# The LRU's gates from high and low halves in fp32r, three tiles of mLSTM's convolution and the chain of softplus placed among them, and the row of x's factors one step later

## The chip, the cores and the metric

One NeuronCore of a Trainium2 chip runs the whole program. The metric is the device time of one execution in microseconds, as the median over the runs. TensorE (PE) multiplies matrices; VectorE (DVE), ScalarE (ACT) and GpSimd (POOL) work element by element; SyncE (SP) issues nearly all DMA transfers.

## The reference

One layer of a decoder trunk with 256 tokens of width 2048. `h = RMSNorm(x)`, then one projection `h @ w_in`, whose columns feed three groups of heads:

```
xc = causal_conv4(xb)                          # A: RG-LRU, 512 channels in 4 blocks of 128
r  = sigmoid(block_diag(xc, wa) + ba)          # recurrence gate
i  = sigmoid(block_diag(xc, wx) + bx)          # input gate
log_a = -8 * r * softplus(-lam)
a, u = exp(log_a), sqrt(-expm1(2 * log_a)) * (i * xc)
h_t = a_t * h_(t-1) + u_t;   y_lru = h * silu(zb)

uc = silu(causal_conv4(u))                     # B: mLSTM, 768 channels, 4 heads
q, k = block_diag(uc, wq), block_diag(uc, wk);  v = block_diag(u, wv)
...                                            # gates, stabilised matrix memory, norm
...                                            # C: MoBA attention, 768 channels, 6 heads
```

The three outputs are joined, projected by `w_out` and added to `x`; then cross-attention into 256 memory tokens, and a final RMSNorm. All tensors are float32.

## The kernel before, in words

**Weights.** The weight columns are cut into groups (`GROUPS`), and each group into chunks along the 2048 inputs (`CHUNKS`, numbered on through the program): lx is chunks 0 to 7, u0 8 to 11, u2 12 to 15, u4 16 to 19, lz0 20 to 23, o0 24 to 31, o1 32 to 39, lz2 40 to 43, then q, k and the rest. `load` (L162) issues a chunk's DMA on SP's queue into one of four `raw` buffers. `split` (L179) makes two fp32r halves of it: ACT copies the high half `wh` (L204), DVE subtracts it from `raw` for the low half `wl` (recorded at L150, in the helper `tt`). Six buffers hold each half. `mm` (L252) multiplies the chunk: for the groups of channels (lx, u, lz, q, k) a matmul of `wh` with x's high and low halves side by side, 512 columns (L272), and one of `wl` with x's high half, 256 columns (L276); for o, z and v three matmuls with the weights as the moving operand (L292 to L294).

**Order.** The main loop (L1193) goes chunk by chunk: it first records the splits of chunks up to four ahead, with the loads that follow, then `mm(i)`, then what hangs on a finished group (`done`, L1128), then one `step` of a queue of generators. Each generator is a piece of the work beside the projections; it runs up to its next `yield` in one step, so a `yield` decides behind which chunk's matmuls the next piece stands. `done` puts evacuations in front of the queue and other work behind it. Each engine executes its own instructions in the recorded order, and waits on the others by semaphores.

**The work that the change touches.** After lx the queue holds two empty steps, `stats("x")` (L432), `lru_scale`, `u_scale`, `softplus_lam` and `lru_core`. `stats` makes the factors `1/rms` of the tokens, as two diagonal matrices `d_x` (DVE, L450), two steps later multiplies them with ones on PE (L455) so that a row of factors stands in every partition (`rrow`), and `lru_scale` (L501) and `u_scale` (L576) multiply the LRU's input and u0 by it on POOL. `softplus_lam` (L392) is a small Exp on ACT and a chain of some 18 short dependent operations on DVE (`log1p`, L376). `lru_core` (L508) convolves four tiles of 128 channels, one per step: an Identity on ACT with the first tap and the bias (L512), three multiply-adds on DVE (recorded at L153, helper `stt`). Then it makes the gates: per tile two f32 matmuls on PE, with `lw`, whose DMA is issued at chunk 6 (L519, L520), and two Sigmoids, two tiles per step; then Exp and Tanh, the products, a Sqrt and the scans. `ml_conv` (L580) is the same convolution for mLSTM, six tiles in six steps, queued when u4 is done; then three Silu, two empty steps, and `ml_qkv`.

Of the kernel before, what the change touches and what calls it, by code (L numbers as in the profile page):

```python
# [9 lines left out]
F32 = mybir.dt.float32  # L10
# [96 lines left out]
def kernel(ctx: ExitStack, tc: tile.TileContext, xT, memT, x, mem, ws, vec_d, lw_d, fg_d, out):  # L107
# [234 lines left out]
    def expand(name, blk):  # L342
        t = bdp.tile([128, 6, 128], F32, name=f"bd_{name}", tag="bd")
        bd[name] = t
        for c in range(6):
            G.tensor_tensor(t[:, c, :].rearrange("p (b o) -> p b o", o=4), dmask,
                            blk(c)[:, None, :].to_broadcast([128, 32, 4]), OP.mult)

    def late_consts():
        G.memset(dmask, 1.0)  # L350
# [40 lines left out]

    def softplus_lam():  # L392
        lam = vc("lam", 0, 4)
        e, m = small("sp_e", 4), small("sp_m", 4)
        stt(e, lam, -1.0, lam, OP.mult, OP.max)
        S.activation(e, e, AF.Exp, scale=-1.0)
        log1p(sp8, e, "sp")
        V.tensor_scalar(m, lam, -1.0, 0.0, op0=OP.mult, op1=OP.max)
        tt(sp8, sp8, m, OP.add)
        V.tensor_scalar(sp8, sp8, 8.0, None, op0=OP.mult)  # L400
        V.tensor_scalar(nsp8, sp8, -1.0, None, op0=OP.mult)
# [30 lines left out]
    def stats(which):  # L432
# [18 lines left out]
        yield  # L451
        yield
        p = ps()
        for i in range(2):
# [46 lines left out]
    def lru_scale():  # L501
        xp = L["xp"]
        for b in range(2):
            v = xp[:, 2 * b:2 * b + 2, 3:259]
            G.tensor_tensor(v, v, rb("x"), OP.mult)
        yield

    def lru_core():  # L508
        xp = L["xp"]
        xc = big(2, 4, 256)  # L510
        for c in range(4):
            S.activation(xc[:, c, :], xp[:, c, 0:256], AF.Identity, scale=vc("cw", 4 * c), bias=vc("cb", c))  # L512
            for j in range(1, 4):
                stt(xc[:, c, :], xp[:, c, j:j + 256], vc("cw", 4 * c + j), xc[:, c, :], OP.mult, OP.add)
            yield
        r, ig = big(3, 4, 256), big(4, 4, 256)
        for c in range(4):
            p = ps()
            P.matmul(p[:, :256], lw[:, c, :], xc[:, c, :], start=True, stop=True)  # L519
            P.matmul(p[:, 256:], lw[:, 4 + c, :], xc[:, c, :], start=True, stop=True)  # L520
            S.activation(r[:, c, :], p[:, :256], AF.Sigmoid, bias=vc("ba", c))
            S.activation(ig[:, c, :], p[:, 256:], AF.Sigmoid, bias=vc("bx", c))
            if c % 2:
                yield
        aa, th = big(5, 4, 256), big(6, 4, 256)
        for c in range(4):
            S.activation(aa[:, c, :], r[:, c, :], AF.Exp, scale=nsp8[:, c:c + 1])
            S.activation(th[:, c, :], r[:, c, :], AF.Tanh, scale=sp8[:, c:c + 1])
            if c % 2:
                yield  # L530
        tt(r, aa, aa, OP.mult)
# [554 lines left out]
    def bg(*gens):  # L1086
        queue.extend(gens)
# [105 lines left out]
    for i in range(NS):  # L1193
# [94 lines left out]
```

## Time and profile before

| what | value |
|---|---|
| median of 3 runs | 517.29 us (517.17 to 517.47) |
| the profiled execution's own time | 518.01 us |
| its span, first to last instruction | 516.3 us |
| PE busy | 505.4 us, 98% of the span, 2682 matmul passes |
| DVE busy | 345.5 us, 67% |
| ACT busy | 301.0 us, 58% |
| POOL busy | 62.7 us, 12% |
| mean granted TensorE clock | 0.997 |
| read from HBM | 96.15 MB, 190 GB/s over the span |

Times in the profile count from the first instruction. The profiled execution is one execution; its own time is 0.72 us over the median of the runs. A share of busy time is a mean over stages: where PE is busy without a break, the other engines' idle time costs nothing; what counts for them is whether a result is there when PE's next matmul wants it.

### The profile page before, as it was taken

The numbers are of one execution on the slowest core, as the hardware profiler recorded it, in microseconds if no ns is written. First come the engines' busy times: TensorE is split into PE (matmuls) and PEld (weight loads), VectorE is DVE, ScalarE is ACT, GpSimd is POOL, SyncE is SP. The second block draws the span as 40 slices with busy tenths as digits, with TensorE's granted clock in tenths as the row PEclk, the third lists the DMA queues.
The fourth block names the chain that finished last, engine by engine and source line by source line (L and its number), as shares of the span: only waits on it lengthen the run. The fifth ranks groups of instructions, "written<-read, shape, count | busy, mean of one in ns | idle before, by whom it ended". The sixth has DMA issues, their size and how long they took to land.

```text
span 516.3 us, 7381 instructions
## 1 busy us (share of the span) xinstructions
PE 505.4 (98%) x2682; PEld 439.9 (85%) x2682; DVE 345.5 (67%) x562; ACT 301.0 (58%) x500; POOL 62.7 (12%) x76
## 2 busy tenths in 40 slices
PE   8999999999999999999999999999999999999994
PEld 6887889988888888889988888888888888888883
DVE  6858964797468755747745566654667857748774
ACT  5775678688663533343555766445647657748444
POOL 1714112000150210001000000000250011000000
PEclk9999999999999999999999999999999999999998
DMA  8997454566645655436753364688675554643704
GB/s 278 398 344 232 140 156 126 169 208 221 214 146 167 189 170 164 120 125 188 247 176 124 119 206 165 193 300 299 206 254 174 180 188 164 203 164 101 266 2 163
DMA packets 31508, 98.73 MB, mean 191 GB/s; under 512 B 3568, under 2 KB 4720, under 8 KB 31472
## 3 DMA queue, kind: packets, MB, share of 16 engines
q1 hardware_dynamic: 30896, 97.59, 57.2%
q10 hardware_dynamic: 576, 0.66, 0.4%
q8 instruction: 21, 0.34, 0.3%
q14 instruction: 15, 0.12, 0.1%
HBM read 96.15 MB, written 2.10 MB: 190 GB/s over the span
## 4 chain that ended last, share of the span: by engine, by line
PE 88%; DVE 4%; ACT 3%; issue 2%; DMA 1%; POOL 1%; ACTq 0%; DVEq 0%; POOLq 0%
PE acc_out L292 6%; PE acc_out L294 6%; PE acc_out L293 6%; PE acc_k L272 4%; PE acc_q L272 4%; PE acc_z L294 4%; PE acc_z L292 4%; PE acc_z L293 4%; PE acc_cq L272 3%; PE acc_ck L272 3%; PE acc_lz L272 3%; PE acc_lx L272 3%; PE acc_u L272 3%; PE acc_q L276 2%; PE acc_k L276 2%; PE acc_v L293 2%
## 5 line engine op out<-in xcount | busy, mean ns | idle before, releaser
L150 DVE TENSOR_TENSOR wl<-raw,wh 128x1024 fp32r<-128x1024 f32 (+4 forms) x169 | 199.7, 1195 | 97.2 <-ACT wh L204 90.9
L204 ACT ACTIVATE wh<-raw 128x1024 fp32r<-128x1024 f32 (+2 forms) x160 | 158.9, 1013 | 32.9 <-DMA raw<-ws 15.4
L292 PE MATMUL acc_out<-wh,a_y 128*128 128x512 f32 x128 | 50.8, 397 | 0.0
L294 PE MATMUL acc_out<-wh,a_y 128*128 128x512 f32 x128 | 50.0, 390 | 0.0
L293 PE MATMUL acc_out<-wl,a_y 128*128 128x512 f32 x128 | 49.8, 389 | 0.0
L292 PE MATMUL acc_z<-wh,a_x 128*128 128x512 f32 x96 | 39.6, 413 | 0.0
L294 PE MATMUL acc_z<-wh,a_x 128*128 128x512 f32 x96 | 37.6, 392 | 0.0
L293 PE MATMUL acc_z<-wl,a_x 128*128 128x512 f32 x96 | 37.5, 390 | 0.0
L272 PE MATMUL acc_k<-a_x,wh 128*128 128x512 f32 x96 | 34.5, 402 | 0.0
L272 PE MATMUL acc_q<-a_x,wh 128*128 128x512 f32 x96 | 34.4, 400 | 0.0
L476 POOL TENSOR_TENSOR w<-ev,rrow 128x512 f32<-128x512 f32 x10 | 16.9, 1692 | 133.4 <-DVE ev L150 120.4
L294 PEld LDWEIGHTS acc_out<-wh,a_y 128*128 128x128 f32 x128 | 24.0, 188 | 5.2
L293 PEld LDWEIGHTS acc_out<-wl,a_y 128*128 128x128 f32 x128 | 24.1, 188 | 4.7
L292 PEld LDWEIGHTS acc_out<-wh,a_y 128*128 128x128 f32 x128 | 24.0, 188 | 4.6
L276 PE MATMUL acc_q<-a_x,wl 128*128 128x256 f32 x96 | 26.9, 280 | 0.0
L276 PE MATMUL acc_k<-a_x,wl 128*128 128x256 f32 x96 | 26.8, 279 | 0.0
L417 POOL TENSOR_TENSOR mask<-mask,yt 128x512 f32<-128x512 f32 x7 | 10.1, 1444 | 129.6 <-ACT yt L416 129.6
L272 PE MATMUL acc_lz<-a_x,wh 128*128 128x512 f32 x64 | 23.5, 408 | 0.0
L272 PE MATMUL acc_lx<-a_x,wh 128*128 128x512 f32 x64 | 22.1, 396 | 1.1 <-ACT wh L193 1.0
L272 PE MATMUL acc_ck<-a_m,wh 128*128 128x512 f32 x64 | 22.9, 401 | 0.0
L272 PE MATMUL acc_cq<-a_h,wh 128*128 128x512 f32 x64 | 22.7, 399 | 0.0
L272 PE MATMUL acc_u<-a_x,wh 128*128 128x512 f32 x64 | 22.6, 398 | 0.0
(328 smaller groups left out, 1161.8 us busy)
## 6 DMA issues: line engine op xcount, KB each, us to landing
raw<-ws SPq DMA_DIRECT2D x138, 512.0 KB, 3.9
raw<-ws SPq DMA_DIRECT2D x24, 384.0 KB, 3.1
w<-x SPq DMA_DIRECT2D x8, 512.0 KB, 7.7
raw<-ws SPq DMA_DIRECT2D x8, 392.0 KB, 3.3
w<-memT SPq DMA_DIRECT2D x8, 256.0 KB, 5.2
w<-xT SPq DMA_DIRECT2D x7, 256.0 KB, 5.5
out<-xg SPq DMA_DIRECT2D x5, 256.0 KB, 2.8
w<-fg SPq DMA_DIRECT2D x2, 512.0 KB, 4.7
```

The costliest lines, as they stand in the source:

```text
L150: V.tensor_tensor(out, a, b, op)
L204: S.activation(h[:, :kc * n], r[:, :kc * n], AF.Copy)
L272: P.matmul(a[m], h[:, kk * n + m * 128:kk * n + m * 128 + 128], both, start=first, stop=False, skip_group_check=True)
L276: P.matmul(a[m][:, :256], l[:, kk * n + m * 128:kk * n + m * 128 + 128], xh, start=False, stop=last, skip_group_check=True)
L292: P.matmul(o, xh[:, sl], mh, start=first, stop=False)
L293: P.matmul(o, xh[:, sl], ml, start=False, stop=False)
L294: P.matmul(o, xl[:, sl], mh, start=False, stop=last)
L417: G.tensor_tensor(sq[which], sq[which], q, OP.add)
L476: G.tensor_tensor(dst, e, rb(which), OP.mult)
```

## The change

`stats("x")` has one more empty step ahead of its matmul, and `lru_scale` no longer ends a step of its own, so that `u_scale` follows in the same one. `softplus_lam` is cut in two: its Exp stays where it was, the chain on DVE moves behind the gates of the LRU's tiles 0 and 1. `lw` gets a high half (copy on ACT) and a low half (subtraction on DVE), recorded after chunk 11; each convolved tile of the LRU gets the same two halves right behind its convolution; the gates are three fp32r matmuls each, high by high, high by low and low by high, in place of one f32 matmul. Tiles 0, 1 and 2 of mLSTM's convolution move out of `ml_conv` into the three steps of `lru_core` with the gates of tiles 2 and 3 and with the Exps; `ml_conv` does tiles 3 to 5. The four new pairs of halves take four of the eight buffers that hold y's halves later.

```diff
+    def halves_tile(name):
+        return acts.tile([128, 2, 2, 256], F32R, tag="y", name=name)
...
-    def softplus_lam():
-        lam = vc("lam", 0, 4)
-        e, m = small("sp_e", 4), small("sp_m", 4)
+    def softplus_exp():
+        lam, e = vc("lam", 0, 4), small("sp_e", 4)
         stt(e, lam, -1.0, lam, OP.mult, OP.max)
         S.activation(e, e, AF.Exp, scale=-1.0)
-        log1p(sp8, e, "sp")
+        L["sp_e"] = e
+
+    def softplus_lam():
+        lam, m = vc("lam", 0, 4), small("sp_m", 4)
+        log1p(sp8, L["sp_e"], "sp")
...
         yield
         yield
+        if which == "x":
+            yield
         p = ps()
         for i in range(2):
             P.matmul(p[:, :256], ones_r, d[:, i].rearrange("p a b -> p (a b)"), start=i == 0, stop=i == 1)
...
             G.tensor_tensor(v, v, rb("x"), OP.mult)
-        yield
+        return
+        yield
+
+    def lw_halves():
+        h, l = (halves_tile(n).rearrange("p a b c -> p (a b c)").rearrange("p (a b) -> p a b", a=8)
+                for n in ("lw_h", "lw_l"))
+        S.activation(h, lw, AF.Copy)
+        tt(l, lw, h.bitcast(F32), OP.subtract)
+        L["lw"] = h, l
 
     def lru_core():
         xp = L["xp"]
         xc = big(2, 4, 256)
+        lwh, lwl = L["lw"]
+        xs = [halves_tile(f"xc{j}") for j in range(2)]
         for c in range(4):
             S.activation(xc[:, c, :], xp[:, c, 0:256], AF.Identity, scale=vc("cw", 4 * c), bias=vc("cb", c))
             for j in range(1, 4):
                 stt(xc[:, c, :], xp[:, c, j:j + 256], vc("cw", 4 * c + j), xc[:, c, :], OP.mult, OP.add)
+            h, l = (xs[c // 2][:, c % 2, i, :] for i in range(2))
+            S.activation(h, xc[:, c, :], AF.Copy)
+            tt(l, xc[:, c, :], h.bitcast(F32), OP.subtract)
             yield
         r, ig = big(3, 4, 256), big(4, 4, 256)
         for c in range(4):
             p = ps()
-            P.matmul(p[:, :256], lw[:, c, :], xc[:, c, :], start=True, stop=True)
-            P.matmul(p[:, 256:], lw[:, 4 + c, :], xc[:, c, :], start=True, stop=True)
+            h, l = (xs[c // 2][:, c % 2, i, :] for i in range(2))
+            for i in range(2):
+                o, k = p[:, 256 * i:256 * i + 256], 4 * i + c
+                P.matmul(o, lwh[:, k, :], h, start=i == 0, stop=False, skip_group_check=True)
+                P.matmul(o, lwh[:, k, :], l, start=False, stop=False, skip_group_check=True)
+                P.matmul(o, lwl[:, k, :], h, start=False, stop=True, skip_group_check=True)
             S.activation(r[:, c, :], p[:, :256], AF.Sigmoid, bias=vc("ba", c))
             S.activation(ig[:, c, :], p[:, 256:], AF.Sigmoid, bias=vc("bx", c))
-            if c % 2:
+            if c == 1:
+                softplus_lam()
+                yield
+            elif c == 3:
+                ml_conv_tile(0)
                 yield
...
             S.activation(th[:, c, :], r[:, c, :], AF.Tanh, scale=sp8[:, c:c + 1])
             if c % 2:
+                ml_conv_tile(1 + c // 2)
                 yield
...
-        for c in range(6):
-            S.activation(uc[:, c, :], u[:, c, 0:256], AF.Identity, scale=vc("mcw", 4 * c), bias=vc("mcb", c))
-            for j in range(1, 4):
-                stt(uc[:, c, :], u[:, c, j:j + 256], vc("mcw", 4 * c + j), uc[:, c, :], OP.mult, OP.add)
+        uc = M["uc"]
+        for c in range(3, 6):
+            ml_conv_tile(c)
             yield
...
-            bg(idle(2), stats("x"), lru_scale(), u_scale(), call(softplus_lam), lru_core())
+            bg(idle(2), stats("x"), lru_scale(), u_scale(), call(softplus_exp), lru_core())
...
+        if i == 11:
+            lw_halves()
```

The order on the engines shows three places. First, ACT's instructions from the LRU's tile 1 to tile 3; `w2` is the convolved tensor, `xc0` and `xc1` hold the halves of its tiles. Before:

```order
L512 ACTIVATE w2_657<-w1_435,vec_90 128x256
L204 ACTIVATE wh21_718<-raw21_592 128x1024
L512 ACTIVATE w2_657<-w1_435,vec_90 128x256
L204 ACTIVATE wh22_744<-raw22_615 128x1024
L512 ACTIVATE w2_657<-w1_435,vec_90 128x256
L204 ACTIVATE wh23_770<-raw23_666 128x1024
```

and in the changed kernel:

```order
L531 ACTIVATE w2_640<-w1_435,vec_90 128x256
L535 ACTIVATE xc0_641<-w2_640 128x256
L204 ACTIVATE wh21_707<-raw21_589 128x1024
L531 ACTIVATE w2_640<-w1_435,vec_90 128x256
L535 ACTIVATE xc1_642<-w2_640 128x256
L204 ACTIVATE wh22_735<-raw22_619 128x1024
L531 ACTIVATE w2_640<-w1_435,vec_90 128x256
L535 ACTIVATE xc1_642<-w2_640 128x256
L204 ACTIVATE wh23_763<-raw23_653 128x1024
```

Between the Identity of a tile and the next `wh` there is now the copy of the convolved tile, which reads what DVE's three multiply-adds leave. Second, DVE's instructions of the same stretch. Before:

```order
L153 SCALAR_TENSOR_TENSOR w2_657<-w1_435,vec_90,w2_657 128x256 x3
L150 TENSOR_TENSOR wl21_719<-raw21_592,wh21_718 128x1024
L153 SCALAR_TENSOR_TENSOR w2_657<-w1_435,vec_90,w2_657 128x256 x3
L150 TENSOR_TENSOR wl22_745<-raw22_615,wh22_744 128x1024
L153 SCALAR_TENSOR_TENSOR w2_657<-w1_435,vec_90,w2_657 128x256 x3
L150 TENSOR_TENSOR wl23_771<-raw23_666,wh23_770 128x1024
```

and in the changed kernel:

```order
L153 SCALAR_TENSOR_TENSOR w2_640<-w1_435,vec_90,w2_640 128x256 x3
L150 TENSOR_TENSOR xc0_641<-w2_640,xc0_641 128x256
L150 TENSOR_TENSOR wl21_708<-raw21_589,wh21_707 128x1024
L153 SCALAR_TENSOR_TENSOR w2_640<-w1_435,vec_90,w2_640 128x256 x3
L150 TENSOR_TENSOR xc1_642<-w2_640,xc1_642 128x256
L150 TENSOR_TENSOR wl22_736<-raw22_619,wh22_735 128x1024
L153 SCALAR_TENSOR_TENSOR w2_640<-w1_435,vec_90,w2_640 128x256 x3
L150 TENSOR_TENSOR xc1_642<-w2_640,xc1_642 128x256
L150 TENSOR_TENSOR wl23_764<-raw23_653,wh23_763 128x1024
```

A subtraction that needs ACT's copy stands between each convolution and the next `wl`. Third, DVE's instructions in o0, from the low half of chunk 28 to that of chunk 31 (`w3`, `w5` are the LRU's gate and its Exp, `w7` and `w8` mLSTM's input and its convolution). Before:

```order
L150 TENSOR_TENSOR wl28_924<-raw28_802,wh28_923 128x784
L150 TENSOR_TENSOR wl29_945<-raw29_838,wh29_944 128x784
L150 TENSOR_TENSOR wl30_967<-raw30_870,wh30_966 128x784
L150 TENSOR_TENSOR w3_822<-w5_888 128x1024
L150 TENSOR_TENSOR wl31_986<-raw31_898,wh31_985 128x784
```

and in the changed kernel:

```order
L150 TENSOR_TENSOR wl28_963<-raw28_795,wh28_962 128x784
L150 TENSOR_TENSOR wl29_984<-raw29_860,wh29_983 128x784
L153 SCALAR_TENSOR_TENSOR w8_896<-w7_554,vec_90,w8_896 128x256 x3
L150 TENSOR_TENSOR wl30_1010<-raw30_905,wh30_1009 128x784
L150 TENSOR_TENSOR w3_815<-w5_923 128x1024
L150 TENSOR_TENSOR wl31_1029<-raw31_937,wh31_1028 128x784
```

Tile 2 of mLSTM's convolution now stands ahead of the low half of chunk 30; tiles 0 and 1 stand in the same way ahead of chunks 26 and 27.

## Rows read from the trace of the kernel before

**Rows 1.** The page, busy time of the engines over the whole execution: us, share of the span, instructions. PE is TensorE's matmuls.
```profile
PE 505.4 (98%) x2682; PEld 439.9 (85%) x2682; DVE 345.5 (67%) x562; ACT 301.0 (58%) x500; POOL 62.7 (12%) x76
```

**Rows 2.** Busy time of each engine by stretch. Columns: from and to in us, length, then busy us and instructions of PE, PEld (weight loads), DVE, ACT, POOL, the granted TensorE clock (1.00 is full), the DMA share and GB/s. The stretches are u2 with u4 and the start of lz0; o0; o1; and from the first Sigmoid of the LRU to the high half of chunk 30.
```profile
42.00:66.90 24.90, 23.83 (x134) 20.28 (x133) 22.96 (x50) 14.48 (x23) 8.54 (x5) 1.00 0.54 173
78.70:95.80 17.10, 17.10 (x99) 17.10 (x98) 10.46 (x12) 13.17 (x20) 3.11 (x5) 1.00 0.48 140
95.80:113.10 17.30, 17.30 (x98) 16.57 (x97) 15.29 (x27) 12.01 (x17) 0.00 (x0) 1.00 0.58 174
68.00:86.77 18.77, 18.77 (x106) 17.45 (x105) 7.86 (x11) 15.48 (x27) 5.09 (x6) 1.00 0.50 145
```

**Rows 3.** PE in order of time at the matmul of x's factors (L455). Columns of this and the groups of single engines below: start in us, duration in us, engine, line, operation, out<-in by the program's names, shapes, count, and in brackets the idle time of the engine just before and what ended it.
```profile
42.38 0.28 PE L276 MATMUL acc_u<-a_x,wl 128*128 128x256 f32 x1
43.72 0.78 PE L455 MATMUL ps<-d_x,ones_r 128*128 128x256 f32 x2 [1.06 <-DVE d_x L450]
44.33 0.39 PE L272 MATMUL acc_u<-a_x,wh 128*128 128x512 f32 x1
```

**Rows 4.** PE in order of time at the start of o1's sixth chunk (106.22) and of lz2's first chunk (113.09).
```profile
106.22 0.34 PE L292 MATMUL acc_o<-wh,a_x 128*128 128x384 f32 x1
106.45 0.45 PE L293 MATMUL acc_o<-wl,a_x 128*128 128x384 f32 x1
...
113.09 0.40 PE L272 MATMUL acc_lz<-a_x,wh 128*128 128x512 f32 x1
113.63 0.39 PE L276 MATMUL acc_lz<-a_x,wl 128*128 128x256 f32 x1
```

**Rows 5.** PE in order of time, the gate matmuls of tile c = 2 (71.44) and the first of c = 3 (72.30); a row of x2 is one f32 matmul in its two passes.
```profile
71.44 0.59 PE L519 MATMUL ps<-w,w 128*128 128x256 f32 x2
...
72.30 0.59 PE L519 MATMUL ps<-w,w 128*128 128x256 f32 x2
```

**Rows 6.** PE in order of time, cross attention's scores: the first of twelve 256-column fp32r matmuls (L952 to L954) and the first matmul behind them.
```profile
459.35 0.28 PE L952 MATMUL ps<-w,cqh 128*128 128x256 f32 x1
...
460.77 0.39 PE L292 MATMUL acc_cv<-wh,a_m 128*128 128x512 f32 x1
```

**Rows 7.** The first split of a weight quarter, 256 columns: the high half on ACT (L193) and the low half on DVE.
```profile
3.82 0.42 ACT L193 ACTIVATE wh<-raw 128x256 fp32r<-128x256 f32 x1 [1.55 <-DMA raw<-ws]
...
4.36 0.42 DVE L150 TENSOR_TENSOR wl<-raw,wh 128x256 fp32r<-128x256 f32 x1
```

**Rows 8.** DVE in order of time from u2 to lz0: low halves `wl`, the first operation of softplus (L380), the convolution of the LRU's four tiles (L153, three steps each), the sums of u2 (`ev`).
```profile
45.78 5.91 DVE L150 TENSOR_TENSOR wl<-raw,wh 128x1024 fp32r<-128x1024 f32 x3
...
52.04 0.17 DVE L380 TENSOR_SCALAR sp_q<-sp_e 128x4 f32<-128x4 f32 x1 [0.27 <-ACT sp_e L396]
...
55.19 1.52 DVE L153 SCALAR_TENSOR_TENSOR w<-w,vec,w 128x256 f32<-128x256 f32 x3
...
57.75 0.75 DVE L150 TENSOR_TENSOR ev<-acc_u,ev 128x256 f32<-128x256 f32 x2
...
59.55 2.55 DVE L153 SCALAR_TENSOR_TENSOR w<-w,vec,w 128x256 f32<-128x256 f32 x3
62.02 1.22 DVE L150 TENSOR_TENSOR wl<-raw,wh 128x1024 fp32r<-128x1024 f32 x1
63.16 1.52 DVE L153 SCALAR_TENSOR_TENSOR w<-w,vec,w 128x256 f32<-128x256 f32 x3
...
65.73 1.52 DVE L153 SCALAR_TENSOR_TENSOR w<-w,vec,w 128x256 f32<-128x256 f32 x3
```

**Rows 9.** ACT in order of time: the Identity of the LRU's tile 3 (L512), u4's evacuation (L468), a table load, the first Sigmoid (L521), lz0's Silu (L551), and the high halves of chunks 30 to 32.
```profile
57.71 0.59 ACT L512 ACTIVATE w<-w,vec 128x256 f32<-128x256 f32 x1
...
64.02 0.69 ACT L468 ACTIVATE ev<-acc_u 128x256 f32<-128x256 f32 x2 [1.67 <-PE acc_u L276]
...
65.47 1.28 ACT L521 ACT_TABLE_LOAD   x1
...
68.00 0.47 ACT L521 ACTIVATE w<-ps,vec 128x256 f32<-128x256 f32 x1 [1.25 <-PE ps L520]
...
82.46 0.63 ACT L551 ACTIVATE w<-w 128x512 f32<-128x512 f32 x1 [1.11 <-POOL w L476]
...
86.77 0.84 ACT L204 ACTIVATE wh<-raw 128x784 fp32r<-128x784 f32 x1
```

**Rows 10.** POOL (GpSimd) in order of time: the products with the row of x's factors, of the LRU's input (L505) and of u0 (L577).
```profile
44.99 3.39 POOL L505 TENSOR_TENSOR w<-w,rrow 128x512 f32<-128x512 f32 x2 [2.12 <-ACT rrow L458]
48.34 2.28 POOL L577 TENSOR_TENSOR w<-ev,rrow 128x512 f32<-128x512 f32 x1
```

**Rows 11.** PE in order of time, the first matmul of chunk 30 (the seventh of o0).
```profile
91.53 0.34 PE L292 MATMUL acc_o<-wh,a_x 128*128 128x392 f32 x1
```

**Rows 12.** DVE in order of time: the low halves of chunks 30, 35, 36 and 37.
```profile
87.65 0.97 DVE L150 TENSOR_TENSOR wl<-raw,wh 128x784 fp32r<-128x784 f32 x1 [2.80 <-ACT wh L204]
...
100.20 0.93 DVE L150 TENSOR_TENSOR wl<-raw,wh 128x768 fp32r<-128x768 f32 x1
...
103.13 0.96 DVE L150 TENSOR_TENSOR wl<-raw,wh 128x768 fp32r<-128x768 f32 x1 [1.72 <-ACT wh L204]
...
105.44 0.95 DVE L150 TENSOR_TENSOR wl<-raw,wh 128x768 fp32r<-128x768 f32 x1
```

**Rows 13.** PE in order of time, the warm-up: four f32 matmuls in eight passes of 256 columns at the start of the run.
```profile
0.82 3.65 PE L328 MATMUL ps<-const-float32-1.0 128*128 128x256 f32 x8 [0.82 <-PEq L1281]
```

More of the change, by code (lines that the diff above doesn't have):

```diff
@@ L578, in u_scale, with ml_conv_tile @@
         yield
-    def ml_conv():
-        u, uc = M["u"], big(8, 6, 256)
-        M["uc"] = uc
-        for c in range(6):
-            S.activation(uc[:, c, :], u[:, c, 0:256], AF.Identity, scale=vc("mcw", 4 * c), bias=vc("mcb", c))
-            for j in range(1, 4):
-                stt(uc[:, c, :], u[:, c, j:j + 256], vc("mcw", 4 * c + j), uc[:, c, :], OP.mult, OP.add)
+    def ml_conv_tile(c):
+        if c == 0:
+            M["uc"] = big(8, 6, 256)
+        u, uc = M["u"], M["uc"]
+        S.activation(uc[:, c, :], u[:, c, 0:256], AF.Identity, scale=vc("mcw", 4 * c), bias=vc("mcb", c))
+        for j in range(1, 4):
+            stt(uc[:, c, :], u[:, c, j:j + 256], vc("mcw", 4 * c + j), uc[:, c, :], OP.mult, OP.add)
+    def ml_conv():
+        uc = M["uc"]
+        for c in range(3, 6):
+            ml_conv_tile(c)
             yield
```

## Prediction

> **What bounds the kernel now.** I read the page's busy times first, then split the part that the change touches by stage. The matmul engine PE is busy for 505.4 of 516.3 us [rows 1], so the time moves only by PE's own work and by the waits between its matmuls. From 42 to 66.9 us (groups u2, u4, the start of lz0) VectorE (DVE) is busy for 22.96 of 24.90 us, ScalarE (ACT) for only 14.48 [rows 2]: DVE is nearly full, and it prepares the low half `wl` of each weight chunk that PE multiplies next. In o0 (78.7 to 95.8) DVE has room, in o1 (95.8 to 113.1) it is at 15.29 of 17.30. What the reader is to see: PE hardly waits, but its supplier has a margin of a few microseconds, in just the stage where the change adds work.
>
> Two places cost PE something now. At 42.4 it waits for the diagonal factors `d_x`: from the start of the matmul ahead of L455 to the one behind it, three steps, 42.38 to 44.33 pass, 1.95 us, where 3 x 0.118 would do: 1.6 us lost [rows 3]. In o1 PE waits for `wl` at four chunk bounds: 0.23 and then 0.28 between starts at 106.22, where 0.17 is usual, and 0.54 instead of 0.23 at 113.09 [rows 4]; with 108.47 and 110.78, of the same kind, the sum is 1.0 us.
>
> **What the change takes away.** The row of x's factors: `d_x` is ready just ahead of the 43.72 start of L455; the new place is behind u2's second chunk, near 45.3, so the 1.6 us go. `lru_scale` gives its step back, and all later steps stay where they were. The gates: eight f32 matmuls of two passes each; the two of c = 2 take 71.44 to 72.30, 0.43 each [rows 5], 3.45 us for all. After: 24 of the 256-column fp32r form, of which twelve take 459.35 to 460.77, 0.118 each [rows 6]: 2.83 us. Gain 0.6 us. By the Trainium skill, "TensorE: Matmul & The Clock Gate", Back-to-back issue gap, 256 columns should take an estimated 109 ns, which would make the 24 matmuls 2.6 us and the gain 0.8; the rows show 118 ns and decide. So PE has 2.2 us less.
>
> **What it adds on the way to PE.** ACT copies a high half of `lw` (like a `wh`) and of each conv tile (128x256 fp32r: 0.42), and DVE subtracts (`lw_l` at the pitch of a `wl`, 1.14; a tile 0.42) [rows 7, 8]. By busy time that is little, and softplus, 52.04 to 55.19 on DVE, goes out of the way [rows 8]. What counts is the order. Now ACT runs ahead: its Identity for tile 3 is done at 58.3 though DVE convolves tile 3 from 65.73 [rows 8, 9]; a round of DVE, conv and `wl`, takes 63.16 to 65.73, 2.57 us, less than PE's 2.8 per chunk. After, the copy of a tile stands on ACT ahead of the next `wh` and waits for DVE's conv; so `wh` starts only after conv and copy, DVE's `wl` waits for it, and nothing overlaps. One round: conv 1.52, wake and copy 0.45, `wh` 1.05, `wl` at its pitch 1.14: 4.15 us.
>
> I walk it on the clock of before. DVE ends `wl` 15 at 45.2 and `lw_l` at 46.3, u0's two sums at 47.0. The factors reach POOL at 46.5 instead of 44.99; its three products take 5.6 us in turn with DVE's three `wl`, each holding the other up: 5.91 us for three that need 3.4 alone [rows 8, 10]. DVE is through near 53.3; `sp_e` and its Exp bring the first conv at 54.3 (55.19 before: softplus is gone, `lw_l` and the later factors eat most of that). Round one has u2's sums and a second `wl`: 4.15 + 0.67 + 1.14 = 6.0. Round two meets POOL's product of u2, which stretched the three conv steps at 59.55 from 1.52 to 2.55 [rows 8]: 5.2. Round three 4.15; then tile 3 needs conv, copy and subtraction, 2.45. Sum: 54.3 + 6.0 + 5.2 + 4.15 + 2.45 = 72.1 for the low half of tile 3. PE wants it for the gates of c = 3: 72.30 before [rows 5], less 1.6, less 0.45 for the quicker matmuls ahead of it, 70.25. **First new wait: 1.9 us.** Bounds: 0.9 if POOL's product falls outside the rounds, 2.9 if two fall in.
>
> **The lateness goes on.** ACT is late too: behind the last copy (from 71.2) stand `wh` 23, u4's evacuation, `wh` 24 and a table load, so the first Sigmoid comes at 71.2 + 0.4 + 0.95 + 0.55 + 0.75 + 1.28 = 75.2; it stood at 68.00, where it waited for PE [rows 9]. From there to `wh` 30 (86.77) ACT has 15.48 us of work [rows 2, 9], and the three early conv tiles add three Identities at a pitch of 0.50: 92.2. The Silu in between waits for POOL's product of lz0, 1.1 us [rows 9]: 93.3. DVE then has conv tile 2 ahead of `wl` 30: 93.4 + 1.5 + 0.97 = 95.85. PE wants `wl` 30 0.18 after the start of its chunk: 91.53 + 0.18 [rows 11], less 2.2, plus 1.9: 91.4. **Second: 4.4 us**, spread over the chunks of o0, whose 2.13 us are shorter than u's. Bounds: 2.2 if the Silu does not wait and DVE gets `wl` 30 out at once; 5.3 if the first wait is at its upper end.
>
> From there DVE has no margin. In before it took 87.65 to 100.20 from `wl` 30 to `wl` 35 [rows 12], 12.55 us for five chunks that PE does in 10.5, and lived off what it had in hand; without that the tail of the LRU (three products, a Sqrt by way of ACT, the scans) costs 2.0. Then 2.93 to `wl` 36 and 2.31 to `wl` 37, against 2.09 each: 1.06 more; behind them the matmuls of `ml_qkv`, now in o1, give DVE 0.87 per chunk and the series ends. **Third: 3.06 less the old 1.0, 2.05 us net.** Bounds: 0 and 2.6. The weight loads stand in the same order on SP's queue, four chunks ahead, and hide.
>
> **Sum**: -1.6 - 0.6 + 1.9 + 4.4 + 2.05 = +6.1. Against the profiled execution's own 518.01 (span 516.3) that is 524.1; it lies 0.7 over the median 517.29, so I put the median at **523.3 us**, slower by 1.2%.
>
> **Rivals.** (a) *Faster: the margin swallows it.* Chunks are split four ahead, 11 us of PE's work in u4 and lz0; if the rounds of DVE stay near 2.8 us, PE meets no wait, and o1's 1.0 goes too, with three tiles less there: 3.2 less, 514.1. It decides at a low half of tile 3 by 70.25. Against it: the order puts the copy ahead of `wh`, and 4.15 a round follows from rows. 6%. (b) *Only the gates wait*; o0 and o1 recover in DVE's free time (10.46 busy of 17.10 in o0 [rows 2]): -2.2 + 1.9, 517.0, no change. Against it: in o0 it is ACT, 13.17 of 17.10, that is late. 6%. (c) *Gates and o0 wait, o1 no more than now*: -2.2 + 1.9 + 4.4 = +4.1, 521.4. For it: while PE waits in o0, the tail may catch up. 18%. (d) *The clock falls in the new waits.* The granted clock stayed at 1.00, 2.4 GHz, over the stretch with the 1.06 us wait [rows 2, 3], yet this run has no several such waits within 25 us. At 1.2 GHz every matmul takes twice as long, as the first of the run do: eight f32 passes in 3.65 us [rows 13], where two take 0.43 in the gates. 2 us of PE's work at that rate adds 2 us: 525.3. 5%. The Trainium skill, "TensorE: Matmul & The Clock Gate", HAM oscillation, describes a kernel whose array fell back to half clock in each wait for data; by that rule 525.3 would be the time, and the trace so far does not bear it out from 42 us on.
>
> **How the numbers follow.** My forecast, within 522.2 to 524.6, has 57%; (c) 18, (d) 5, (a) 6, (b) 6; the other 8 lie between 518.5 and 521, one of the later waits being half its size. Slower by over 0.2% (about what a measurement of this kernel can tell from no change): 57 + 18 + 5 + 8 = 88. The 12 of (a) and (b) are split as 7 faster and 5 within 0.2%, since (b) lies near the edge. The range takes in (c), the third term at 0 with the second in mid-range, and (d): 519.4 to 525.3.
>
> **What would show it.** Right: no wait at the factors' matmul; 0.118 per gate matmul; a wait of PE of 1 to 3 us on the low half of a conv tile at the gates of c = 2 or 3; ACT idle ahead of each copy until DVE's conv ends; waits of PE on `wh` and `wl` in o0, the longest at its sixth or seventh chunk, then in o1; from 120 us on the same intervals as before. Wrong: PE without waits between 44 and 114, or a round of DVE near 3 us; on the other side, a granted clock under 1.00 there.

## The result and the profile after

The changed kernel takes 524.11 us in the median (523.46 to 525.11, 4 runs) beside 517.23 for the kernel before: a ratio of 1.0139 with a 95% interval of 1.0126 to 1.0152, slower by 6.9 us. (517.29, the median used in the forecast, is that of the first three of these four runs.) The forecast was 523.3 with a range of 519.4 to 525.3. The profiled execution took 523.46 (span 521.4); that of before 518.01 (span 516.3).

The stretches of [rows 2], with lz0 between the first two (columns as there):

```profile
42.00:66.90 24.90, 24.90 (x148) 21.80 (x147) 21.20 (x31) 10.20 (x17) 8.18 (x4) 1.00 0.46 159
66.90:78.70 11.80, 11.79 (x72) 10.45 (x71) 9.89 (x27) 9.53 (x19) 1.98 (x1) 1.00 0.34 102
78.70:95.80 17.10, 13.39 (x71) 12.01 (x70) 10.88 (x18) 14.08 (x23) 3.11 (x5) 1.00 0.42 118
95.80:113.10 17.30, 16.57 (x83) 15.65 (x83) 14.31 (x21) 11.30 (x16) 0.00 (x0) 0.90 0.55 167
```

PE has no gap left from 42 to 66.9 (24.90 of 24.90; before 23.83), but in the window of the old o0, 78.7 to 95.8, it is busy for 13.39 of 17.10 us where it was never idle; o0 itself now lasts from 77.20 to 100.73. In the last row the granted clock is 0.90: a part of that stretch ran at half clock.

PE in order of time at the gates of tiles 2 and 3, at the waits of o0, and behind them (columns as in [rows 3]):

```profile
70.56 0.28 PE L544 MATMUL ps<-xc,lw_h 128*128 128x256 f32 x1
70.85 0.39 PE L545 MATMUL ps<-xc,lw_h 128*128 128x256 f32 x1
71.07 0.28 PE L546 MATMUL ps<-xc,lw_l 128*128 128x256 f32 x1
...
83.70 0.34 PE L292 MATMUL acc_o<-wh,a_x 128*128 128x392 f32 x1
84.91 0.45 PE L293 MATMUL acc_o<-wl,a_x 128*128 128x392 f32 x1 [0.87 <-DVE wl L150]
...
90.03 0.45 PE L293 MATMUL acc_o<-wl,a_x 128*128 128x392 f32 x1 [0.56 <-DVE wl L150]
...
91.91 0.34 PE L294 MATMUL acc_o<-wh,a_x 128*128 128x392 f32 x1
93.28 0.45 PE L292 MATMUL acc_o<-wh,a_x 128*128 128x392 f32 x1 [1.03 <-ACT wh L204]
94.98 0.44 PE L293 MATMUL acc_o<-wl,a_x 128*128 128x392 f32 x1 [1.25 <-DVE wl L150]
...
98.73 0.53 PE L292 MATMUL acc_o<-wh,a_x 128*128 128x392 f32 x1
99.06 0.53 PE L293 MATMUL acc_o<-wl,a_x 128*128 128x392 f32 x1
```

Read the starts. The low half of a conv tile (70.85) came 0.17 late, 0.28 with its successor. In o0, where 0.18 lies between two starts, 1.21 lie at 83.70, 1.37 at 91.91 and 1.70 at 93.28; with 0.91 ahead of 90.03 PE loses 4.9 us in all. At 98.73 the step from start to start is 0.33 where it was 0.18; the granted clock there is 0.50, shown with the last run.

ACT in order of time: the copy of tile 3 and the next `wh`; the first Sigmoid (L547); lz0's Silu (L582); the Identity of mLSTM's tile 2 (L615); `wh` 30 to 32 in one row.

```profile
69.91 0.42 ACT L535 ACTIVATE xc<-w 128x256 fp32r<-128x256 f32 x1 [2.24 <-DVE w L153]
70.24 1.04 ACT L204 ACTIVATE wh<-raw 128x1024 fp32r<-128x1024 f32 x1
...
73.88 0.48 ACT L547 ACTIVATE w<-ps,vec 128x256 f32<-128x256 f32 x1
...
87.58 0.63 ACT L582 ACTIVATE w<-w 128x512 f32<-128x512 f32 x1 [1.84 <-POOL w L485]
...
91.89 0.58 ACT L615 ACTIVATE w<-w,vec 128x256 f32<-128x256 f32 x1
92.39 2.32 ACT L204 ACTIVATE wh<-raw 128x784 fp32r<-128x784 f32 x3
```

DVE in order of time: the LRU's convolution of tiles 0, 2 and 3 and the subtraction of tile 3; mLSTM's tile 2 and `wl` 30.

```profile
53.22 1.53 DVE L153 SCALAR_TENSOR_TENSOR w<-w,vec,w 128x256 f32<-128x256 f32 x3 [0.77 <-ACT w L531]
...
64.26 1.52 DVE L153 SCALAR_TENSOR_TENSOR w<-w,vec,w 128x256 f32<-128x256 f32 x3
...
68.36 1.52 DVE L153 SCALAR_TENSOR_TENSOR w<-w,vec,w 128x256 f32<-128x256 f32 x3
70.36 0.43 DVE L150 TENSOR_TENSOR xc<-w,xc 128x256 fp32r<-128x256 f32 x1 [0.49 <-ACT xc L535]
...
92.51 1.53 DVE L153 SCALAR_TENSOR_TENSOR w<-w,vec,w 128x256 f32<-128x256 f32 x3 [2.54 <-ACT w L615]
93.95 0.97 DVE L150 TENSOR_TENSOR wl<-raw,wh 128x784 fp32r<-128x784 f32 x1
```

The round without POOL takes 68.36 - 64.26 = 4.10 us, and ACT stands still for 2.24 us ahead of the copy.

### The profile page after: what moved, and what is told of

Read it like the earlier page. It is cut to its first block, busy times and chain, and to the rows that moved or that the text cites. A ratio compares the mean times of both kernels' runs of the same rounds, so it can differ in the third digit from the quotient of the medians.

```text
span 521.4 us, 7408 instructions
## 1 busy us (share of the span) xinstructions
PE 507.4 (97%) x2690; PEld 441.2 (85%) x2690; DVE 352.4 (68%) x567; ACT 303.6 (58%) x505; POOL 63.4 (12%) x76
## 2 busy tenths in 40 slices
DMA packets 31508, 98.73 MB, mean 189 GB/s; under 512 B 3568, under 2 KB 4720, under 8 KB 31472
## 4 chain that ended last, share of the span: by engine, by line
PE 91%; DMA 2%; ACT 2%; DVE 2%; issue 1%; SPq 0%; ACTq 0%; DVEq 0%
PE acc_out L292 6%; PE acc_out L294 6%; PE acc_out L293 6%; PE acc_q L272 4%; PE acc_k L272 4%; PE acc_z L294 4%; PE acc_z L292 4%; PE acc_z L293 4%; PE acc_u L272 3%; PE acc_cq L272 3%; PE acc_ck L272 3%; PE acc_lz L272 3%; PE acc_lx L272 2%; DMA raw<-ws 2%; PE acc_q L276 2%; PE acc_k L276 2%
## 5 line engine op out<-in xcount | busy, mean ns | idle before, releaser
L293 PE MATMUL acc_o<-wl,a_x 128*128 128x392 f32 (+1 forms) x64 | 23.1, 360 | 3.4 <-DVE wl L150 3.4
L292 PE MATMUL acc_o<-wh,a_x 128*128 128x392 f32 (+1 forms) x64 | 22.7, 355 | 1.0 <-ACT wh L204 1.0
```

The lines of the kernel that those rows point to most:

```text
L292: P.matmul(o, xh[:, sl], mh, start=first, stop=False)
L293: P.matmul(o, xh[:, sl], ml, start=False, stop=False)
```

## The experiments

Stage lengths tell the runs apart. **A** is from the first matmul of u0 to that of o0, **B** from there to the first of o1 (the eight chunks of o0), **C** from there to the first of v0, some 230 us into the run. Each is worked out from starts of PE rows of the one profiled execution; the median is over the runs. Each ratio is to runs of the kernel before that were made beside that group, with medians of 517.23 us for the changed kernel, 517.14 for e1 to e4 and 516.92 for e5 to e8.

| kernel | A | B | C | median us | ratio to before (95%) |
|---|---|---|---|---|---|
| before / once more | 39.00 / 38.50 | 17.07 / 17.08 | 134.07 / 134.20 | 517.23 | |
| changed / once more | 37.30 / 37.08 | 23.53 / 22.00 | 134.25 / 135.80 | 524.11 | 1.0139 (1.0126 to 1.0152) |
| e1_factors | 37.09 | 17.07 | 134.15 | 516.44 | 0.999 (0.998 to 1.000) |
| e2_gates | 39.39 | 19.15 | 137.02 | 523.98 | 1.0139 (1.0122 to 1.0156) |
| e3_f32_gates | 37.45 | 17.07 | 135.74 | 518.42 | 1.0022 (1.0009 to 1.0035) |
| e4_conv_back | 37.60 | 19.15 | 136.84 | 521.58 | 1.0089 (1.0074 to 1.0104) |
| e5_pipelined | 36.87 | 17.18 | 135.82 | 518.15 | 1.0023 (1.0013 to 1.0034) |
| e6_softplus | 37.09 | 17.07 | 134.19 | 516.77 | 0.9994 (0.9981 to 1.0007) |
| e7_busy | 37.10 | 21.98 | 135.81 | 523.98 | 1.0135 (1.0114 to 1.0157) |
| e8_pipelined_conv | 36.65 | 17.08 | 132.70 | 514.86 | 0.9960 (0.9947 to 0.9974) |

The theory is that of the prediction: the copy of a convolved tile, placed on ACT ahead of the next `wh`, puts ACT and DVE into rounds of over 4 us; ACT comes late into o0, and DVE has no margin in o1. The rival is that the moved work, mLSTM's tiles and softplus, fills DVE and ACT in o0.

**e1_factors**, only the row of x's factors:

```diff
         yield
         yield
+        if which == "x":
+            yield
         p = ps()
...
             G.tensor_tensor(v, v, rb("x"), OP.mult)
-        yield
+        return
+        yield
```

> The kernel before with the row of x's factors one step later, and nothing else of the change. Theory (the first term of the sum): the 1.6 us at 42.4 go and PE meets nothing new, so 517.3 - 1.6 = 515.7 us; a part of o1's 1.0 may go or stay. Rival (PE comes 1.6 us earlier into o1, where it lives off DVE, and waits there instead): 517.0 or more, with waits of 2 us or more in o1.

Measured 516.44 beside 517.14 in that comparison: 0.7 us faster, not 1.6. Nothing new waits (B and C are as before), so the rival falls. A is shorter by 1.9 than in the one profile and by 1.4 than in the other; the medians say less. The place that the step was sized by differs from one execution to the next, which the last two runs take up.

**e2_gates**, the halves and the fp32r gates alone; the factors, softplus and the tiles of mLSTM's convolution stay in their old places:

```diff
+            h, l = (xs[c // 2][:, c % 2, i, :] for i in range(2))
+            S.activation(h, xc[:, c, :], AF.Copy)
+            tt(l, xc[:, c, :], h.bitcast(F32), OP.subtract)
             yield
...
-            P.matmul(p[:, :256], lw[:, c, :], xc[:, c, :], start=True, stop=True)
-            P.matmul(p[:, 256:], lw[:, 4 + c, :], xc[:, c, :], start=True, stop=True)
+            h, l = (xs[c // 2][:, c % 2, i, :] for i in range(2))
+            for i in range(2):
+                o, k = p[:, 256 * i:256 * i + 256], 4 * i + c
+                P.matmul(o, lwh[:, k, :], h, start=i == 0, stop=False, skip_group_check=True)
+                P.matmul(o, lwh[:, k, :], l, start=False, stop=False, skip_group_check=True)
+                P.matmul(o, lwl[:, k, :], h, start=False, stop=True, skip_group_check=True)
...
+        if i == 11:
+            lw_halves()
```

> The kernel before with the halves and the fp32r gates alone: the factors, softplus and all six tiles of mLSTM's convolution stand where they stood before. Theory (ACT's copy ahead of the next wh makes rounds of 4.1 us and ACT late): softplus and lw_l put the LRU's first convolution near 56.3 (53.2 in the changed kernel), PE arrives 1.6 later, so the gates wait 0.3 + 3.1 - 1.6 = 1.8 us; wh 30 comes at 92.4 + 3.1 - 1.5 (no Identities of mLSTM) = 94.0 and wl 30 near 95.0, wanted at 91.1, so 3.9 us in all with the gates' 1.8; o1 adds 0 to 1.0. Sum -0.6 + 3.9 + 0 to 1.0: 520.5 to 521.6 us. Rival (the moved convolution and softplus make the loss, the halves none): 517.3 - 0.6 = 516.7 us.

523.98 us, all of the loss and 7 us from the rival's time: the halves, with the gates that read them, make the kernel as slow as the whole change. The gates' wait is 2.0 us by PE's starts, 1.8 expected; B grew by 2.08, the 2.1 expected. Its PE rows at these waits (L541 is the gate matmul that reads a tile's high half):

```profile
72.12 0.38 PE L541 MATMUL ps<-xc,lw_h 128*128 128x256 f32 x1 [1.39 <-ACT xc L532]
...
92.86 0.45 PE L292 MATMUL acc_o<-wh,a_x 128*128 128x392 f32 x1 [0.53 <-ACT wh L204]
93.87 0.44 PE L293 MATMUL acc_o<-wl,a_x 128*128 128x392 f32 x1 [0.56 <-DVE wl L150]
```

What I had too small is o1: C is 2.95 longer, where I had 0 to 1.0.

**e3_f32_gates**, the changed kernel with the diff of e2 taken back:

```diff
-            S.activation(h, xc[:, c, :], AF.Copy)
-            tt(l, xc[:, c, :], h.bitcast(F32), OP.subtract)
             yield
...
+            P.matmul(p[:, :256], lw[:, c, :], xc[:, c, :], start=True, stop=True)
+            P.matmul(p[:, 256:], lw[:, 4 + c, :], xc[:, c, :], start=True, stop=True)
```

> The changed kernel with the f32 gates of before and none of the halves; factors, softplus and the three tiles of mLSTM's convolution as in the change. Theory (the halves make ACT late): no rounds; the first Sigmoid waits for PE again near 66.5, wh 30 stands at 86.8 - 1.6 + 1.5 = 86.7 and wl 30 near 89.2 to 90.1, wanted near 90.1, so no wait in o0; o1's old 1.0 partly goes with three tiles. 517.3 - 1.6 - 0 to 1.0 = 514.7 to 515.7 us, granted clock 1.00 throughout o0 and o1. Rival (the three tiles and softplus in o0 are what makes PE wait there): waits of 3 us or more in o0, 518.5 us or more.

B is 17.07 as before: no wait in o0 and no fall of the clock, as the theory has it. But 518.42 is slower than before, not faster, because o1 waits. DVE of this kernel, `wl` 29, mLSTM's tile 2, and the low halves of chunks 30, 33 and 35:

```profile
84.36 0.97 DVE L150 TENSOR_TENSOR wl<-raw,wh 128x784 fp32r<-128x784 f32 x1 [2.59 <-ACT wh L204]
87.87 1.53 DVE L153 SCALAR_TENSOR_TENSOR w<-w,vec,w 128x256 f32<-128x256 f32 x3 [2.54 <-ACT w L606]
89.31 0.97 DVE L150 TENSOR_TENSOR wl<-raw,wh 128x784 fp32r<-128x784 f32 x1
...
96.64 0.96 DVE L150 TENSOR_TENSOR wl<-raw,wh 128x768 fp32r<-128x768 f32 x1 [1.20 <-ACT wh L204]
...
101.87 0.93 DVE L150 TENSOR_TENSOR wl<-raw,wh 128x768 fp32r<-128x768 f32 x1
```

and PE where it waits for the low halves of chunks 33 and 35, 0.94 and 1.08 us behind the start ahead of them, where 0.17 is usual:

```profile
97.65 0.44 PE L293 MATMUL acc_o<-wl,a_x 128*128 128x384 f32 x1 [0.55 <-DVE wl L150]
...
102.85 0.44 PE L293 MATMUL acc_o<-wl,a_x 128*128 128x384 f32 x1 [0.75 <-DVE wl L150]
```

Together with the waits at chunks 36 and 37 PE loses 3.0 us at `wl` in o1, 0.9 in the kernel before by the same count of starts. From `wl` 30 to `wl` 35 it takes 101.87 - 89.31 = 12.56 us, the 12.55 of [rows 12]. The stretch costs DVE the same in both kernels; what differs is the margin with which it enters. Before, `wl` 30 was done 3 us ahead of its matmul [rows 11, 12]; here it is done at 90.3, and chunk 30, whose low half PE wants 13.0 us after o0's start at 77.53, wants it at 90.5. Of the margin of 3.1, 2.85 are gone, and 2.1 of them come out in o1. Part of the delay is ACT's: DVE waited 2.54 us for the Identity of tile 2, which stands ahead of `wh` 30 there.

**e4_conv_back**, the changed kernel with all six tiles of mLSTM's convolution in `ml_conv`:

```diff
             elif c == 3:
-                ml_conv_tile(0)
                 yield
...
-                ml_conv_tile(1 + c // 2)
                 yield
...
-        for c in range(3, 6):
+        for c in range(6):
             ml_conv_tile(c)
             yield
```

> The changed kernel with all six tiles of mLSTM's convolution back in their old steps; halves, fp32r gates, factors and softplus as in the change. Theory (both the late ACT and the three tiles make the wait in o0): wh 30 comes 1.5 us earlier without three Identities, wl 30 another 1.5 without tile 2 ahead of it, so o0's 4.9 us shrink to about 1.9; o1 has its old waits again, 1.0 to 2.5; the clock stays at 1.00, if its fall needs the 3 us in which PE did one matmul. -2.2 + 0.3 + 1.9 + 0 to 1.5 over the old 1.0: 517.3 to 518.8 us. Rival 1 (the tiles are the whole cause): 517.3 - 2.2 + 0.3 = 515.4. Rival 2 (the late ACT alone is): o0 keeps 4.9 and the fall of the clock, 522 or more.

B is 19.15, 2.08 over before, where 1.9 was expected: of the 4.9 us of o0 the late ACT makes 2.1 by itself. The three tiles add the other 2.8 only on top of it: without the halves, in e3, they cost o0 nothing. The time, 521.58, lies between both rivals, but over the expected range, again by o1: C is 2.77 longer.

**e5_pipelined**, nothing but the place of the halves:

```diff
+        def halves(c):
+            h, l = (xs[c // 2][:, c % 2, i, :] for i in range(2))
+            S.activation(h, xc[:, c, :], AF.Copy)
+            tt(l, xc[:, c, :], h.bitcast(F32), OP.subtract)
+
         for c in range(4):
...
-            h, l = (xs[c // 2][:, c % 2, i, :] for i in range(2))
-            S.activation(h, xc[:, c, :], AF.Copy)
-            tt(l, xc[:, c, :], h.bitcast(F32), OP.subtract)
             yield
+            halves(c)
         r, ig = big(3, 4, 256), big(4, 4, 256)
```

> The changed kernel with the halves of each convolved tile recorded one step later, ahead of the next tile's Identity: ACT then writes the next wh before it waits for the convolution. Theory (the order copy, then wh makes ACT late): a round is conv 1.52, wl 1.14, subtraction 0.35, some 3.0 us in place of 4.1; ACT is in time for lz0, o0 has no wait, and the clock stays at 1.00; the gates wait 0 to 1.4 us, since the last tile's halves come behind u4's evacuation; o1 keeps the 2.8 us that the kernel with f32 gates had, since tile 2 still stands ahead of wl 30. That kernel's 518.4, less 0.6, plus 0 to 1.4: 517.8 to 519.2 us. Rival (what makes ACT late is the number of copies, or DVE's extra work, and not their place): waits of 2 us or more in o0, 521 us or more.

518.15 us: 6.0 of the 6.9 us are back, with the same instructions in another order. ACT at tiles 2 and 3 (L533 is the copy of the tile before, L537 the Identity):

```profile
63.52 0.42 ACT L533 ACTIVATE xc<-w 128x256 fp32r<-128x256 f32 x1 [1.04 <-DVE w L153]
63.85 0.59 ACT L537 ACTIVATE w<-w,vec 128x256 f32<-128x256 f32 x1
64.34 1.05 ACT L204 ACTIVATE wh<-raw 128x1024 fp32r<-128x1024 f32 x1
...
66.57 0.41 ACT L533 ACTIVATE xc<-w 128x256 fp32r<-128x256 f32 x1
67.00 1.28 ACT L551 ACT_TABLE_LOAD   x1
68.29 0.47 ACT L551 ACTIVATE w<-ps,vec 128x256 f32<-128x256 f32 x1
```

A copy waits 1.04 or nothing instead of 2.24, the next comes 3.05 us later, and the first Sigmoid at 68.29 stands 5.6 us ahead of the changed kernel's 73.88. B is 17.18, within 0.1 of before, and the gates wait 0.3 us; the rival on the number of copies falls. The run moves each copy together with its subtraction on DVE, so which of the two had to move was not tested alone; ACT's idle time of 2.24 us ahead of a copy, ended by DVE's convolution, is what speaks for the copy.

**e6_softplus**, e3 with the diff of e4 as well: f32 gates, and all tiles of mLSTM's convolution in `ml_conv`.

> The kernel before with the factors' row one step later and softplus behind the gates of tiles 0 and 1; f32 gates, all six tiles of mLSTM's convolution in their old steps. Against the kernel with f32 gates and three moved tiles (518.4 us) only the tiles differ, against that with the factors alone (516.4 us) only softplus. Theory (tile 2 ahead of wl 30 takes DVE's margin, and o1's 2.8 us follow from it): no waits in o1 beyond 0.5 us, 516.4 us. Rival (softplus, 4 us of DVE in lz0, is what makes o1 late): o1 keeps its 2.8 us, 518.4 us.

516.77, and A, B and C as in e1. `wl` 30 has its margin of 3.1 us again (done at 88.0, wanted at 91.1). Softplus in lz0 costs nothing that can be measured; e3's o1 waits come from the three tiles.

**e7_busy**, 21 idle matmuls in the two longest waits:

```diff
+        def keep_busy(n):
+            p = ps()
+            for _ in range(n):
+                P.matmul(p[:, :256], ones_r, act_hi["x"][0][:, 0, :], start=True, stop=True)
+
+        if i == 30:
+            keep_busy(9)
...
                     P.matmul(o, xh[:, sl], mh, start=first, stop=False)
+                    if i == 30 and kk == 0 and t == 0:
+                        keep_busy(12)
                     P.matmul(o, xh[:, sl], ml, start=False, stop=False)
```

> The changed kernel with 21 matmuls more, whose results nobody reads, in the two longest waits: nine ahead of chunk 30's first matmul, twelve behind it, 0.118 us each, so that PE works from 92.1 to 95.0 where it stood still. Theory 1 (the clock fell because PE stood still for most of 91.9 to 95.0, and its 1.6 us came on top): the clock stays at 1.00 and the time falls by 1.6 to 522.5 us. Theory 2 (the clock fell for that, but the slow 3.4 us only took the place of a wait in o1, since DVE was late there anyway): the clock stays at 1.00, o1's chunks 33 and 35 wait 0.8 and more again, 2.8 us in all, and the time stays within 0.7 us of 524.1. Rival (the clock falls for another reason): a granted clock of 0.50 near 96 to 99 again.

523.98 us, unchanged, with a granted clock of 1.00: theory 2. B is 1.55 shorter than in the changed kernel and C 1.56 longer; B + C is 157.79 and 157.78. PE waits 0.81 and 0.90 us at chunks 33 and 35, as theory 2 has it. Whether the idle matmuls kept the clock up is taken up with the last run.

**e8_pipelined_conv**, e5 with all tiles of mLSTM's convolution back, and one line more:

```diff
         for c in range(4):
+            if c == 2:
+                yield
             p = ps()
             h, l = (xs[c // 2][:, c % 2, i, :] for i in range(2))
```

> The changed kernel with three things altered: the halves one step later, as in the run above; all six tiles of mLSTM's convolution in their old steps; and the gates of tiles 2 and 3 one step behind those of 0 and 1, so that the last tile's halves are ready. Theory: neither the gates nor o0 wait, o1 no more than 0.5 us; the factors' 1.2 us and the gates' 0.6 us are both gained: 517.2 - 1.8 = 515.4 us. Rival (the LRU's end, one step later, makes o1 late): 2 us or more of waits in o1, 517.4 us or more.

514.86 us, 0.4% under before and 1.8% under the changed kernel: the whole, without the three moved tiles, pays once the order is right. A is 0.44 shorter than in e1 and e6, near the 0.56 that the fp32r gates save. Its stretches of o0, and of o1 with the start of lz2:

```profile
78.70:96.00 17.30, 17.30 (x99) 17.30 (x98) 10.95 (x12) 14.46 (x22) 2.51 (x5) 1.00 0.58 181
96.00:100.00 4.00, 4.00 (x25) 4.00 (x24) 2.35 (x5) 2.87 (x5) 0.00 (x0) 1.00 0.51 148
100.00:117.00 17.00, 17.00 (x100) 16.28 (x99) 16.55 (x28) 12.64 (x19) 0.00 (x0) 1.00 0.58 198
```

PE has no gap in any. That C is 1.4 shorter than before is more than o1's old waits of 0.9; I did not take the rest apart.

**e9_before_again**, the kernel before, unchanged.

> The kernel before once more, for a second profiled execution of it. The first had the wait for x's factors of 1.6 us; the kernel with the halves alone, which leaves that place as it was, waited 0.3 us there, its DVE being 1.35 us earlier in the stretch that DMA paces. Theory (the wait hangs on how the weights of lx arrive in an execution, and 1.6 is not what it costs in the median): another wait than 1.6 us, between 0 and 2, and a span shorter by about as much as the wait is. Rival (the halves change it, and the kernel before always waits 1.6): 1.5 to 1.7 us again.

PE at the factors' matmul in this execution:

```profile
43.16 0.28 PE L276 MATMUL acc_u<-a_x,wl 128*128 128x256 f32 x1
43.96 0.78 PE L455 MATMUL ps<-d_x,ones_r 128*128 128x256 f32 x2 [0.53 <-DVE d_x L450]
44.58 0.39 PE L272 MATMUL acc_u<-a_x,wh 128*128 128x512 f32 x1
```

The same place in e2, which has not moved it (L462 there):

```profile
42.20 0.28 PE L276 MATMUL acc_u<-a_x,wl 128*128 128x256 f32 x1
42.36 0.78 PE L462 MATMUL ps<-d_x,ones_r 128*128 128x256 f32 x2
42.98 0.39 PE L272 MATMUL acc_u<-a_x,wh 128*128 128x512 f32 x1
```

By the same reckoning as in the prediction (three steps less 0.35) the wait is 1.6 [rows 3], 1.07 and 0.43 us. So it differs by 0.5 us between two executions of one kernel, and the rival falls. It follows how far DVE is behind PE: `wl` 15 starts 4.25, 3.77 and 3.08 us behind u0's first matmul in these three. The third is another kernel, so that its 0.43 is also a matter of the execution is not shown. The time did not get shorter with the wait (518.36 us, span 516.6): PE had come 0.7 us later out of lx. In lx ACT waits 1.2 to 1.5 us for the transfer of each of three chunks in a row (24 to 30 us) in both executions; that the transfers make the difference is not shown.

**e10_after_again**, the changed kernel, unchanged.

> The changed kernel once more, for a second profiled execution. Theory: the gates of tile 2 wait between 0 and 1.9 us, by how far DVE stands ahead at 42 us; whatever they wait, o1 begins at the same distance from wl 30, since DVE and not PE sets it; PE again stands still for most of some 3 us at chunk 30, and the granted clock falls behind it. Rival (the clock's fall was an accident of the one execution): 1.00 throughout.

It took 523.00 us. PE stands still at the same places in o0 for the same times within 0.05 us, but the clock does not fall, as the rival has it. The stretch from 96.4 to 99.4 us, columns as in [rows 2], in the first execution:

```profile
96.40:99.40 3.00, 3.00 (x11) 3.00 (x11) 3.00 (x4) 1.24 (x1) 0.00 (x0) 0.50 0.67 218
```

In the second, 18 matmuls in place of 11, at 1.00:

```profile
96.40:99.40 3.00, 3.00 (x18) 3.00 (x18) 3.00 (x4) 1.69 (x2) 0.00 (x0) 1.00 0.59 209
```

PE of the second execution, the waits at chunk 30 and at chunk 33:

```profile
92.81 0.44 PE L292 MATMUL acc_o<-wh,a_x 128*128 128x392 f32 x1 [1.03 <-ACT wh L204]
94.52 0.45 PE L293 MATMUL acc_o<-wl,a_x 128*128 128x392 f32 x1 [1.26 <-DVE wl L150]
...
100.83 0.45 PE L292 MATMUL acc_o<-wh,a_x 128*128 128x384 f32 x1
101.83 0.44 PE L293 MATMUL acc_o<-wl,a_x 128*128 128x384 f32 x1 [0.55 <-DVE wl L150]
```

Against the first execution its matmuls stand 0.47 us earlier ahead of the slow stretch (92.81 for 93.28), 2.01 earlier at the first of o1 (98.72 for 100.73), and 0.46 earlier again from o1's middle on: B + C is 157.80 beside 157.78. So 1.5 us at half clock cost nothing, since PE waits there for `wl` 33 when the clock stays up (1.00 between starts at 100.83, where 0.17 is usual), and then longer for `wl` 35. e7's clock of 1.00 is thus no proof that the idle matmuls keep the clock up: here it stayed up without them. What keeps or loses it between two such executions stays open.

## Why the prediction came out right, step by step

The direction, the bound and the size were right, and the mechanism stands: e2 has the whole loss with the halves and the gates alone, and e5 gives back 6.0 us by moving the halves alone. Single steps failed. The gates' wait put A 1.4 us too high, and the way from the profile to the median, with the factors' term, was 1.4 us too low: it is in part luck that the median lies within 0.8 us of the forecast.

- **The factors, -1.6.** The wait went, and A shrank by 1.4 to 1.9 in e1; but in medians it is worth 0.7 (e1) or 0.2 (e6). What failed is to take [rows 3] as the kernel's wait: it was 1.6 and 1.07 us in two executions of the kernel before, and 0.43 in e2.
- **The gates, -0.6.** Right: from the first gate matmul to the second matmul behind the group of twelve pass 65.57 to 67.24, 1.67 us, where the group of four f32 ones took 66.94 to 68.89, 1.95: 0.28 for two tiles, 0.56 in all.
- **The gates' wait, +1.9.** Measured 0.28, and 0.17 in the second execution, under the bounds of 0.9 to 2.9. The round of 4.15 us was right (4.10). What failed is first the start of the walk: the first convolution began at 53.22, not 54.3, as DVE was 1.1 us further at the end of lx. The rounds were another 0.2 us shorter than the walk, and PE came to this matmul 0.4 us later, at 70.68 instead of 70.25. `wl` 15, from which the walk goes, in the kernel before:

```profile
43.97 1.22 DVE L150 TENSOR_TENSOR wl<-raw,wh 128x1024 fp32r<-128x1024 f32 x1
```

and in the changed kernel, where nothing ahead of it on DVE is altered:

```profile
42.85 1.22 DVE L150 TENSOR_TENSOR wl<-raw,wh 128x1024 fp32r<-128x1024 f32 x1
```

It is the same shift between DVE and PE that goes with the wait for the factors: 2.95 and 2.74 us in the two executions of the changed kernel, 4.25 and 3.77 in those of before. e2, whose convolution softplus holds back, waits 2.0.
- **o0, +4.4.** Measured 4.9 in both executions, within 2.2 to 5.3. `wl` 30 was ready at 94.9 (95.85 by the walk) and wanted at 90.2 (91.4, which held the 1.9 that did not come). The first Sigmoid at 73.88 and `wh` 30 at 92.39 are 1.3 and 0.9 us ahead of the walk; the Silu's wait for POOL was 1.84, not 1.1.
- **o1, +2.05.** Right, with the clock up. By the starts of PE in the second execution, the low halves of chunks 33 and 35 cost 2.0 us, those of 36 and 37 0.86 and 0.24, where 2.0, 0.84 and 0.22 were forecast; less the 0.9 of before that is 2.2. C grows by 1.73 only (135.80 less 134.07), as what lies behind o1 is a little shorter, and by 2.95 and 2.77 where all tiles stay in `ml_conv` (e2, e4). e3 adds what I had not seen: the three tiles, with tile 2 ahead of `wl` 30, are enough for it, without a late ACT. DVE enters a stretch of 12.55 us that PE does in 10.5, so most of what `wl` 30 loses of its margin of 3 comes out in o1.
- **The sum.** By stretches, forecast and measured: A -0.3 and -1.70, B +4.4 and +6.46 (4.93 without the fall of the clock), C +2.05 and +0.18 (1.73): 6.15 in all, 4.94 measured. The profiled execution, forecast at 524.1, took 523.46. From there to the median I took off the 0.7 by which the profile of before lay over its runs; the changed kernel's lies 0.65 under its own, so that step failed by 1.4, and the median, forecast at 523.3, is 524.11. Why the profiled executions of before lie above its median and those of the changed kernel below is open; the factors' term, 0.9 to 1.4 us smaller in medians than in the profile, is of that size, but that it is the reason is not shown. A sign that I gave did not come: from 120 us on the intervals are not those of before. From lz2 to v0 pass 113.85 us instead of 116.77, since two groups of matmuls of `ml_qkv` now stand in o1; I did not take the rest apart.
- **The rivals.** (a) to (c) fell: o0 and o1 both wait. (d) happened in one of two profiled executions, 0.50 of full clock (1.2 GHz) for some 3.4 us, from 96.2 to 99.6, after PE had begun one matmul between 91.91 and 94.98, and it cost nothing. The price I gave it, slow matmuls added to the time, forgot that PE is not the bound behind such a wait. Nor do [rows 13], its source, show the half clock: the granted clock from 0.8 to 4.2 us is 1.00 in that trace, so why those passes took 0.46 each is open. What half clock costs a matmul here is a step of 0.33 instead of 0.18. The Trainium skill, "TensorE: Matmul & The Clock Gate", HAM oscillation, counts half of the time at half clock as lost; by that the 3.4 us here would cost an estimated 1.7. The trace agrees for o0 and not for the run: against the second execution B is 1.53 longer, and C 1.55 shorter.

## What to carry to other kernels

Before adding a small operation to an engine that prepares the next operand of the bound engine, look at what it must wait for and what is queued behind it: copies of 0.42 us each, with their subtractions, cost 6 to 7 us (e5, e2), as they waited for DVE with the next `wh` behind them; one step later PE waits 0.3 us for them. Ask of each supplier with what margin it enters the stretch in which it is slower than its consumer; here most of a loss ahead of that stretch was paid in it. Size a wait from more than one execution when a transfer paces what is ahead of it.

## What the runs showed of the hardware

The granted clock fell to 0.50 (1.2 GHz) in one execution and stayed at 1.00 in another of the same kernel, with the same two waits at chunk 30 (idle times of 1.03 and 1.25 us, and 1.03 and 1.26). The fall cost nothing over the run, as PE would have waited for DVE in o1 instead: B + C was 157.78 us with it, 157.80 without, and 157.79 where PE was given idle matmuls.

DVE and POOL held each other up also in a small operation: the 128x4 one that begins softplus took 1.28 us (74.00 to 75.28) while POOL multiplied (73.28 to 75.26), and 0.17 us alone [rows 8]; that product of POOL took 1.98 us, its ten of this form 1.30 in the median.
